# Hybrid decoder block on one core: row statistics in the opening, another background order, and two norms in one step

## The chip, the core and the metric

The kernel runs on one core of a Trainium2 chip. The metric is device time in microseconds (us) of one execution; beside the median of several executions there is one execution taken by the hardware profiler. Engines are named as the profile names them: PE (TensorE matmuls; PEld is its weight load), DVE (VectorE), ACT (ScalarE), POOL (GpSimd), SP (SyncE, whose queue issues every DMA of this kernel).

## What is computed

One decoder layer over 2048 positions of width 1024, in float32, then a final norm. Cut to what matters:

```python
h = rmsnorm(x, norm1_g)
proj = h @ w_in                       # q, k, v, g, a, and three conv parts
q, k, v, g, a, cb, cc, ch = split(proj)
log_a = log_sigmoid(a @ w_gate_up + b_gate) / 16       # forget gate
o = rmsnorm(gla_chunked(q, k, v, log_a), gla_norm_g) * silu(g)
o_conv = cb * causal_conv3(cc * ch)
x = x + concat(o, o_conv) @ w_out
h2 = rmsnorm(x, norm2_g)
x = x + (silu(h2 @ w_ffn_gate) * (h2 @ w_ffn_up)) @ w_ffn_down
return rmsnorm(x, norm_f_g)
```

`rmsnorm` divides each position's 1024 values by the root of their mean square and multiplies by a gain per column.

## The kernel before, in words

**Tiling.** Positions are cut into four blocks of 512 (`PB`), two blocks to a "half". Activations lie transposed: a tile `h[k, j]` holds 128 features (k) by the 512 positions of block j. `xt` is x in that layout, `x` the plain one, one position to a row.

**Products.** Every large matmul is done in a unit of seven products instead of eight (`PRODUCTS`, L34): a unit takes 256 output columns and two blocks, and multiplies weight combinations A11, S1, S2, A12, S3, S4, A22 with operand combinations B11, T1, T2, B21, T3, B22, T4. B11 is `h[k, 0]` for k below 4, B12 `h[k, 1]`, B21 and B22 the same for k from 4. T1 = B12 - B11, T2 = B22 - T1, T3 = B22 - B12, T4 = B21 - T2. To keep float32 precision each operand is split (`split`, L145) into a rounded part hi (ACT copy, L146) and a rest lo (DVE subtraction, L147), and each product is three matmuls per k (L328 to L330), so a product is 12 matmuls of 128x512 and a unit 84. POOL forms the weight combinations (L311 to L318). Results leave PSUM by ACT copies (`copied`, L348; `settled`, L377) and DVE additions (`plus`, L352). Within a unit the first accumulator is copied as c11 after product 1, and as c12 after product 3; the second as c22 after product 2. The third product goes on in the accumulator that c11 was copied from, the fifth in that of c12, the sixth in that of c22, so those products wait for the copies.

**The opening.** `first_stats` (L414) loads the 16 tiles of xt of blocks 0 and 1, squares each on ACT, adds the squares up per block (DVE for block 0, POOL for block 1), and `column_rstd` (L160) sums them over partitions with a matmul by ones; the result is 1/rms, repeated on all partitions, in SBUF, 128x512. `build_first` (L255) then scales each tile on DVE (`scaled`, L440), splits it, and does the first unit as eight plain products (L279 to L281): 48 matmuls for block 0 (j = 0), 48 for block 1 (j = 1). After k = 3 of j = 0 block 1's `column_rstd` is issued. Then POOL forms the T's (L288), for one k after another: T1, T2 and T4 overwrite one tile `t1` from pool "b", T3 overwrites `h[k, 1]`.

**Tiles.** Pool "t" has nine tiles of 128x512 and serves block 0's `h`, the c copies, settled results and others; pool "b" has eleven and serves block 1's `h`, the T's, and most background work. "op" has 28 split operands. A tile can be taken again when the last operation that uses its old content is done.

**Background.** While units run, `tick()` after each product takes a step of the first generator in `background`: at every tick while `hurry` is set, at every second otherwise; at `pace % 4 == 1` it takes a step of `ahead` when it takes none of background. At the start the list is: `gate_weights`, `gate(0)` (the forget gates of blocks 0 and 1: 40 matmuls at L497, eight at L513, scans on DVE), `row_stats(2)`, `row_stats(3)` (1/rms of blocks 2 and 3 from rows of x: ACT squares with an accumulated sum, L397, then small operations on 128x4, and four transposes that repeat the result on all partitions, L406 and L407), `unhurried`, `h1_ahead` (operands of the second half, stored to DRAM). `h2_ahead` (L792) does the same for the second half of the feed-forward; it waits two steps, makes one block's norm, waits two more, makes the other's.

**Who sets the order.** The program is written in that order, and a planner that simulates the five engines fixes each engine's order (`TileContext(nc, schedule_with_timeline_sim=True)`, L1096): of what its model holds ready, what stands first in the program goes first. So a later line can run ahead of an earlier one that waits; in the trace the first weight splits (L146, at 13.64 us) run ahead of the Ln of the norm (L170, at 16.78 us) that stands before them. Once fixed, each engine does its instructions in that order. `issue_after` adds an order by hand.

**Activation tables.** `Ln` and `Exp` of the norms and gates need another table in ACT than `Silu`; a load (ACT_TABLE_LOAD) takes 1.283 us in the trace. `act.preload_act_table_set` loads a set that holds both.

Of the kernel before, what the change touches and what calls it, by code (L numbers as in the profile page):

```python
# [10 lines left out]
F32 = mybir.dt.float32  # L11
# [36 lines left out]
def tile_hymba_block(ctx, tc, x, xt, win, wa, wgu, wout, wffn, wdown, wdown_first, small, out):  # L48
# [111 lines left out]
    def column_rstd(ssq, n, rb=None):  # L160

        rb = ssq if rb is None else rb
        tot = bank("tot")
        pe.matmul(tot[:], ones[:], ssq[:], start=True, stop=True)
        finish_rstd(rb, tot, n)
        return rb
# [27 lines left out]
    def unhurried():  # L194
        hurry.clear()
        yield

    def drain_background(until=lambda: False):
        while background and not until():
            step()  # L200


    def split_op(src):
        o = opp.tile([P, 2, PB], F32R, name="op", tag="op")
        split(src, o[:, 0, :], o[:, 1, :])
        return o
# [45 lines left out]
            put("B22", k, b22)  # L252
            yield

    def build_first(quad, w, later):  # L255


        ops = {b: [] for _, b in PRODUCTS}
        h, o = {}, {}
        quarters = ("A11", "A12"), ("A21", "A22")  # L260
        los = []
        for j in range(2):
            for r in range(2):
                o[r, j] = bank()
            for k in range(KD):
                with ExitStack() as stack:
                    if len(los) > 1:
                        stack.enter_context(tc.issue_after(los[-2].ins))
                    h[k, j] = quad(k, j)
                x = opp.tile([P, 2, PB], F32R, name="op", tag="op")  # L270
                los.append(split(h[k, j][:], x[:, 0, :], x[:, 1, :]))
                if (j, k) == (0, 3):
                    rbs[1] = column_rstd(later, D)
                name = ("B11", "B12")[j] if k < 4 else ("B21", "B22")[j]
                ops.setdefault(name, []).append(x)
                c = slice(k % 4 * P, (k % 4 + 1) * P)
                for r in range(2):
                    q = w[quarters[r][k // 4]]
                    pe.matmul(o[r, j][:], q[:, 0, c], x[:, 0, :], start=k == 0, stop=False)  # L279
                    pe.matmul(o[r, j][:], q[:, 0, c], x[:, 1, :], start=False, stop=False)  # L280
                    pe.matmul(o[r, j][:], q[:, 1, c], x[:, 0, :], start=False, stop=k == KD - 1)  # L281
        for k in range(4):
            t1 = bt("t1")
            b11, b12, b21, b22 = h[k, 0], h[k, 1], h[k + 4, 0], h[k + 4, 1]
            for n, y, a, b in (
                ("T1", t1, b12, b11), ("T2", t1, b22, t1), ("T3", b12, b22, b12), ("T4", t1, b21, t1)
            ):
                pool.tensor_tensor(y[:], a[:], b[:], ALU.subtract)  # L288
                ops[n].append(split_op(y[:]))
        return ops, [(r, j, o[r, j], True) for j in range(2) for r in range(2)]  # L290

    def weight_quarter(src):
# [92 lines left out]
        return s  # L385


    rbs = {}

    def row_stats(b):  # L390
        ssq = mtiny.tile([P, PT, 2], F32, name="ssq", tag="ssq")
        for t in range(PT):
            for e in range(2):
                xn = bt("xn")
                r0 = b * PB + t * P
                load(xn[:], x[r0 : r0 + P, e * PB : (e + 1) * PB])
                act.activation(xn[:], xn[:], AF.Square, accum_out=ssq[:, t, e : e + 1])  # L397
            yield
        v, l, y0 = [mtiny.tile([P, PT], F32, name=n, tag=n) for n in ("msq", "rl", "ry")]
        dve.tensor_tensor(v[:], ssq[:, :, 0], ssq[:, :, 1], ALU.add)  # L400
        dve.tensor_scalar(v[:], v[:], 1.0 / D, EPS, ALU.mult, ALU.add)
        rsqrt(v[:], v[:], l[:], y0[:])
        rb_ps = bank("rb_ps")
        for t in range(PT):
            rep = mtiny.tile([P, P], F32, name="rep", tag="rep")
            dve.tensor_copy(rep[:], v[:, t : t + 1].to_broadcast([P, P]))  # L406
            pe.transpose(rb_ps[:, t * P : (t + 1) * P], rep[:], ident[:])  # L407
        rb = bt("rb2")
        act.activation(rb[:], rb_ps[:], AF.Copy)
        store(s_rb[b][:], rb[:])  # L410

    raws, first_weights, last_load = {}, {}, []

    def first_stats():  # L414

        for j in range(2):
            for k in range(KD):
                h = bt("h") if j else tt("h")
                raws[j, k] = h
                last_load[:] = [load(h[:], xt[j, :, k, :])]  # L420
            if j == 0:
                raw = raw_weights(win[0])
        ssq = [tiny.tile([P, PB], F32, name="rb2", tag="rb") for _ in range(2)]
        for j in range(2):
            for k in range(KD):
                if k == 0:
                    act.activation(ssq[j][:], raws[j, k][:], AF.Square)
                else:
                    q = opp.tile([P, 2, PB], F32, name="q", tag="op")
                    act.activation(q[:, 0, :], raws[j, k][:], AF.Square)  # L430
                    add = pool if j else dve
                    add.tensor_tensor(ssq[j][:], ssq[j][:], q[:, 0, :], ALU.add)
            if j == 0:
                rbs[0] = column_rstd(ssq[0], D)
                for n, i in (("A11", 0), ("A21", 3), ("A12", 1), ("A22", 2)):
                    first_weights[n] = weight_quarter(raw[:, i, :])
        return ssq[1]

    def scaled(g, rb, h):
        dve.scalar_tensor_tensor(h[:], h[:], g, rb[:], ALU.mult, ALU.mult)  # L440
# [8 lines left out]
        split(raw[:], w[:, :, 0, :], w[:, :, 1, :])  # L449
        yield  # L450

    def build_h(later):


        def quad(k, j):
            return scaled(col(C_G1 + k), rbs[j], raws[j, k])

        return build_first(quad, first_weights, later)

    def h1_ahead():  # L460

# [330 lines left out]
    def h2_ahead(ssq):  # L792


        rb = []
        for j in range(2):
# [117 lines left out]
    def last_unit(src, ops, b12, y, ssq):  # L914
# [51 lines left out]


    act.preload_act_table_set("natural_log_exp_and_others")
    later = first_stats()
    load(wgu_sb[:], wgu)  # L970
    ops, first = build_h(later)
# [129 lines left out]
```

## Time and profile before

| | us |
|---|---|
| median of 3 runs | 2146.97 |
| lowest, highest | 2140.72, 2151.3 |
| the profiled execution | 2146.09 |
| its span, first to last instruction | 2144.2 |
| PE busy in the span | 2043.6 |
| DVE, ACT, POOL busy | 1452.5, 1012.1, 997.0 |

The mean granted TensorE clock of the profiled execution is 0.989 of full speed. How to read the views: in the busy time by stretch, each row gives a stretch, its length, then for each engine the busy us and the number of instructions, then the granted clock, the busy share of the DMA engines and the GB/s. In the list of waits a row reads: engine, waiting operation and line, what ended the wait, the total, how often, the longest. In the groups a row reads: line, engine, operation, output and inputs, shapes, count, then busy us and mean ns of one, then the idle time in front and what ended it. In the view of a tile or line the three numbers are the shortest, median and longest ns. In the timeline a row begins with the start and the length in us.

### The profile page before, as it was taken

Reading aid. Unit: us, or ns where it says so; the run is one execution under the profiler, and the core shown is the slowest. Engines: PE = TensorE matmul, PEld = TensorE weight load, DVE = VectorE, ACT = ScalarE, POOL = GpSimd, SP = SyncE. Lnnn points to the kernel's source line nnn. Section 1 sums busy time; section 2 is a strip of 40 time slices with the busy share of each in tenths; the row PEclk is TensorE's granted clock in tenths of the full one; section 3 lists DMA queues with packets and bytes.
Section 4 is the critical chain, followed back from the end, with each engine's and each line's share of the span. In section 5 each row is a group of like instructions: output and inputs, shape, how many; then the busy total and the mean of one; then the engine's idle time right before and its main releaser. Section 6 shows DMA issues by size and latency. Waiting matters only on the chain.

```text
span 2144.2 us, 26906 instructions
## 1 busy us (share of the span) xinstructions
PE 2043.6 (95%) x9133; PEld 1651.3 (77%) x9133; DVE 1452.5 (68%) x2034; ACT 1012.1 (47%) x1962; POOL 997.0 (46%) x714
## 2 busy tenths in 40 slices
PE   4899899999999999999999999999999999999996
PEld 2677687887888887788888887787888888887775
DVE  8849965556774486888887664554686677664554
ACT  4555434574544235555454553333454454553344
POOL 4526422122201274655655436774644654445774
PEclk9999999999999999999999999999999999999998
DMA  4259658532577884465464577689455455487662
GB/s 150 76 199 315 218 228 286 156 125 79 166 247 256 309 294 152 167 240 220 172 237 182 185 303 283 254 336 355 157 191 205 154 197 196 172 329 293 266 265 108
DMA packets 189977, 467.64 MB, mean 218 GB/s; under 512 B 19856, under 2 KB 65168, under 8 KB 180112
## 3 DMA queue, kind: packets, MB, share of 16 engines
q1 hardware_dynamic: 189840, 465.93, 59.9%
q8 instruction: 72, 1.18, 0.2%
q14 instruction: 65, 0.53, 0.1%
HBM read 297.03 MB, written 168.82 MB: 217 GB/s over the span
## 4 chain that ended last, share of the span: by engine, by line
PE 70%; DVE 11%; DMA 8%; issue 4%; ACT 3%; POOL 3%; SPq 1%; DVEq 0%; POOLq 0%; ACTq 0%
PE mm L328 20%; PE mm L330 20%; PE mm L329 19%; DVE wq L147 3%; PE mm L722 3%; PE mm L725 3%; PE mm L723 3%; DMA raw<-in_wdown_dram 2%; DVE h L440 2%; DMA raw<-in_wffn_dram 1%; DVE so L147 1%; DVE op L147 1%; DMA op<-shT 1%; DVE c L352 1%; ACT wq L146 1%
## 5 line engine op out<-in xcount | busy, mean ns | idle before, releaser
L328 PE MATMUL mm<-op,wq 128*128 128x512 f32 x2495 | 982.1, 395 | 33.0 <-ACT c L348 20.3
L330 PE MATMUL mm<-op,wq 128*128 128x512 f32 x2495 | 967.6, 392 | 12.4 <-DVE wq L147 11.2
L329 PE MATMUL mm<-op,wq 128*128 128x512 f32 x2495 | 975.6, 391 | 2.5 <-DVE op L147 2.5
L147 DVE TENSOR_TENSOR wq<-raw,wq 128x512 fp32r<-128x512 f32 (+2 forms) x628 | 536.6, 860 | 320.2 <-ACT wq L146 318.3
L146 ACT ACTIVATE wq<-raw 128x512 fp32r<-128x512 f32 (+2 forms) x628 | 367.1, 589 | 566.7 <-PE mm L330 415.4
L328 PEld LDWEIGHTS mm<-op,wq 128*128 128x128 f32 x2495 | 470.4, 189 | 152.1 <-ACT c L348 27.1
L330 PEld LDWEIGHTS mm<-op,wq 128*128 128x128 f32 x2495 | 470.5, 189 | 121.9 <-DVE wq L147 22.4
L329 PEld LDWEIGHTS mm<-op,wq 128*128 128x128 f32 x2495 | 470.7, 189 | 99.8 <-DVE op L147 3.0
L313 POOL TENSOR_TENSOR raw<-s,raw 128x512 f32<-128x512 f32 (+2 forms) x98 | 130.7, 1333 | 437.7 <-DVE wq L147 403.1
L352 DVE TENSOR_TENSOR c<-mm,c 128x512 f32<-128x512 f32 x270 | 185.1, 686 | 100.1 <-PE mm L330 98.0
L311 POOL TENSOR_TENSOR s<-raw 128x512 f32<-128x512 f32 (+2 forms) x98 | 130.8, 1335 | 207.9 <-DMA raw<-in_wffn_dram 96.1
L318 POOL TENSOR_TENSOR raw<-raw 128x512 f32<-128x512 f32 (+2 forms) x98 | 130.4, 1331 | 129.5 <-DVE wq L147 128.9
L348 ACT ACTIVATE c<-mm 128x512 f32<-128x512 f32 x270 | 156.4, 585 | 23.8 <-PE mm L330 23.0
L704 POOL TENSOR_TENSOR ssx<-ssx,q 128x512 f32<-128x512 f32 x52 | 75.2, 1459 | 151.0 <-ACT q L703 151.0
L312 POOL TENSOR_TENSOR raw<-raw 128x512 f32<-128x512 f32 (+2 forms) x98 | 137.2, 1400 | 4.6
L884 POOL TENSOR_TENSOR y<-c,y 128x512 f32<-128x512 f32 x66 | 98.6, 1496 | 67.3 <-DVE c L352 67.2
L147 DVE TENSOR_TENSOR so<-t,so 128x512 fp32r<-128x512 f32 x100 | 89.6, 902 | 23.8 <-ACT so L146 23.6
L722 PE MATMUL mm<-op,wq 128*128 128x512 f32 x256 | 100.9, 394 | 0.0
L723 PE MATMUL mm<-op,wq 128*128 128x512 f32 x256 | 99.7, 390 | 0.0
L146 ACT ACTIVATE wq<-s 128x512 fp32r<-128x512 f32 (+2 forms) x98 | 57.6, 588 | 89.2 <-PE mm L330 86.6
L147 DVE TENSOR_TENSOR wq<-s,wq 128x512 fp32r<-128x512 f32 (+2 forms) x98 | 81.9, 835 | 15.6 <-ACT wq L146 15.2
L146 ACT ACTIVATE so<-t 128x512 fp32r<-128x512 f32 x100 | 62.9, 630 | 48.6 <-DMA sa_B<-so 19.9
(177 smaller groups left out, 1931.2 us busy)
## 6 DMA issues: line engine op xcount, KB each, us to landing
raw<-in_wffn_dram SPq DMA_DIRECT2D x44, 1024.0 KB, 6.1
sa_T<-so SPq DMA_DIRECT2D x88, 512.0 KB, 4.9
op<-sa_T SPq DMA_DIRECT2D x88, 512.0 KB, 9.6
sa_B<-so SPq DMA_DIRECT2D x69, 512.0 KB, 3.4
op<-sa_B SPq DMA_DIRECT2D x69, 512.0 KB, 9.2
raw<-in_win_dram SPq DMA_DIRECT2D x24, 1024.0 KB, 5.7
raw<-in_wdown_dram SPq DMA_DIRECT2D x24, 768.0 KB, 6.1
sx<-y SPq DMA_DIRECT2D x48, 256.0 KB, 3.4
```

The source lines that it names most:

```text
L146: last_hi[:] = [act.activation(hi, src, AF.Copy)]
L147: return dve.tensor_tensor(lo, src, hi.bitcast(F32), ALU.subtract)
L311: pool.tensor_tensor(s1, a21, a22, ALU.add)
L312: pool.tensor_tensor(a21, a11, a21, ALU.subtract)
L313: pool.tensor_tensor(a11, s1, a11, ALU.subtract)
L328: pe.matmul(o[:], wh, xh, start=first and k == 0, stop=False, skip_group_check=True)
L329: pe.matmul(o[:], wh, xl, start=False, stop=False, skip_group_check=True)
L330: return pe.matmul(o[:], wl, xh, start=False, stop=k == n - 1, skip_group_check=True)
L348: act.activation(t[:], o[:], AF.Copy)
L352: dve.tensor_tensor(t[:], o[:], t[:], ALU.add)
L722: pe.matmul(o[e, j][:], wh, m[:, 0, :], start=k == 0, stop=False)
L723: pe.matmul(o[e, j][:], wh, m[:, 1, :], start=False, stop=False)
```

## The change

1. *Opening.* `first_loads` takes the place of `first_stats`: it loads the rows of x of a block (four loads of 128x1024) ahead of the block's xt, and splits the first weight load in four. The mean square comes from one ACT square per row tile with an accumulated sum (`row_squares`), and `rows_rstd`, cut out of `row_stats`, gives 1/rms in a PSUM bank, from which `scaled` reads it. Block 1's squares are issued beside k = 4 to 7 of j = 0, its `rows_rstd` after k = 7.
2. *T operands.* The loop over the four T's is now the outer one, k the inner; T1, T2 and T4 overwrite `h[k, 0]` (pool "t") instead of `t1`.
3. *Background order.* `gate_weights`, six empty steps, `row_stats(2)`, `row_stats(3)`, `gate(0)`, `unhurried`, `h1_ahead`. `row_stats` loads one row tile ahead.
4. *Second feed-forward operands.* `h2_ahead` waits one step, preloads the table, and makes both norms in one step.

The diff, cut to its core:

```diff
+    def pause(n):
+        for _ in range(n):
+            yield
...
-                if (j, k) == (0, 3):
-                    rbs[1] = column_rstd(later, D)
+                if j == 0 and k >= PT:
+                    row_squares(1, k - PT)
...
-        for k in range(4):
-            t1 = bt("t1")
-            b11, b12, b21, b22 = h[k, 0], h[k, 1], h[k + 4, 0], h[k + 4, 1]
-            for n, y, a, b in (
-                ("T1", t1, b12, b11), ("T2", t1, b22, t1), ("T3", b12, b22, b12), ("T4", t1, b21, t1)
-            ):
-                pool.tensor_tensor(y[:], a[:], b[:], ALU.subtract)
-                ops[n].append(split_op(y[:]))
+            if j == 0:
+                rbs[1] = rows_rstd(squares[1])
+        for n, y, a, b in (
+            ("T1", (0, 0), (0, 1), (0, 0)), ("T2", (0, 0), (4, 1), (0, 0)),
+            ("T3", (0, 1), (4, 1), (0, 1)), ("T4", (0, 0), (4, 0), (0, 0)),
+        ):
+            for k in range(4):
+                yy, aa, bb = [h[k + dk, j] for dk, j in (y, a, b)]
+                pool.tensor_tensor(yy[:], aa[:], bb[:], ALU.subtract)
+                ops[n].append(split_op(yy[:]))
...
     def row_stats(b):
         ssq = mtiny.tile([P, PT, 2], F32, name="ssq", tag="ssq")
-        for t in range(PT):
-            for e in range(2):
-                xn = bt("xn")
+
+        def fetch(t):
+            xs = [bt("xn") for _ in range(2)]
+            for e, xn in enumerate(xs):
                 r0 = b * PB + t * P
                 load(xn[:], x[r0 : r0 + P, e * PB : (e + 1) * PB])
+            return xs
+
+        nxt = fetch(0)
+        yield
+        for t in range(PT):
+            xs = nxt
+            if t + 1 < PT:
+                nxt = fetch(t + 1)
+            for e, xn in enumerate(xs):
                 act.activation(xn[:], xn[:], AF.Square, accum_out=ssq[:, t, e : e + 1])
             yield
+        dve.tensor_tensor(ssq[:, :, 0], ssq[:, :, 0], ssq[:, :, 1], ALU.add)
+        rb = bt("rb2")
+        act.activation(rb[:], rows_rstd(ssq)[:], AF.Copy)
+        store(s_rb[b][:], rb[:])
+
+    def rows_rstd(ssq):
+
         v, l, y0 = [mtiny.tile([P, PT], F32, name=n, tag=n) for n in ("msq", "rl", "ry")]
...
             pe.transpose(rb_ps[:, t * P : (t + 1) * P], rep[:], ident[:])
...
+        return rb_ps
...
+    def row_squares(b, t):
+        act.activation(rows[b, t], rows[b, t], AF.Square, accum_out=squares[b][:, t, 0:1])
+
+    def first_loads():
+
+        raw = rawp.tile([P, 4, PB], F32, name="raw", tag="raw")
+        for b in range(2):
+            squares[b] = mtiny.tile([P, PT, 2], F32, name="ssq", tag="ssq")
+            for t in range(PT):
+                xr = opp.tile([P, 2 * PB], F32, name="xr", tag="op")
+                rows[b, t] = xr[:]
+                r0 = b * PB + t * P
+                load(xr[:], x[r0 : r0 + P, :])
             for k in range(KD):
-                h = bt("h") if j else tt("h")
...
+                if b == 0 and k % 4 == 0:
+                    for i in ((0, 3), (1, 2))[k // 4]:
+                        raw_loads.append(load(raw[:, i, :], win[0][:, i, :]))
+                h = bt("h") if b else tt("h")
+                raws[b, k] = h
+                last_load[:] = [load(h[:], xt[b, :, k, :])]
+        for t in range(PT):
+            row_squares(0, t)
+        rbs[0] = rows_rstd(squares[0])
...
     def h2_ahead(ssq):
 
 
-        rb = []
-        for j in range(2):
-            for _ in range(2):
-                yield
-            rb.append(column_rstd(ssq[j], D))
+        yield
+        act.preload_act_table_set("natural_log_exp_and_others")
+        rb = [column_rstd(ssq[j], D) for j in range(2)]
+        yield
...
-        [gate_weights(), gate(0, ops), row_stats(2), row_stats(3), unhurried(), h1_ahead()]
+        [
+            gate_weights(), pause(6), row_stats(2), row_stats(3), gate(0, ops), unhurried(),
+            h1_ahead(),
+        ]
```

More of the change, by code (lines that the diff above doesn't have):

```diff
@@ L407, in row_stats @@
             pe.transpose(rb_ps[:, t * P : (t + 1) * P], rep[:], ident[:])
[L408 to L414, printed above, removed]
-        for j in range(2):
-            for k in range(KD):
-                h = bt("h") if j else tt("h")
[L419 to L437, printed above, removed]
@@ new lines, in rows_rstd @@
+        return rb_ps
+    rbs, raws, first_weights, last_load, rows, squares = {}, {}, {}, [], {}, {}
+    def row_squares(b, t):
[9 more added lines that the diff above has]
+                load(xr[:], x[r0 : r0 + P, :])
+            for k in range(KD):
+                if b == 0 and k % 4 == 0:
[7 more added lines that the diff above has]
+        rbs[0] = rows_rstd(squares[0])
+        for n, i in (("A11", 0), ("A21", 3), ("A12", 1), ("A22", 2)):
+            first_weights[n] = weight_quarter(raw[:, i, :])
```

15 lines of the change are left out of this document (6 added, 9 removed).

## The prediction, made before the changed kernel ran

> **What bounds the kernel now.** I read the page's first part for the engine that fills the span, then the busy time by stretch to find where that engine is not fed.
>
> ```profile
> PE 2043.6 (95%) x9133; PEld 1651.3 (77%) x9133; DVE 1452.5 (68%) x2034; ACT 1012.1 (47%) x1962; POOL 997.0 (46%) x714
> ```
> ```profile
> core 0: us, PE busy (x) PEld busy (x) DVE busy (x) ACT busy (x) POOL busy (x), PEclk, DMA share, GB/s
> 0.00:26.00 26.00, 2.10 (x3) 0.53 (x3) 15.88 (x24) 14.42 (x24) 9.85 (x13) 1.00 0.78 288
> 26.00:42.40 16.40, 14.47 (x50) 10.45 (x50) 16.20 (x20) 5.75 (x10) 5.46 (x4) 1.00 0.00 0
> 42.40:63.00 20.60, 16.40 (x64) 11.20 (x63) 20.33 (x20) 8.12 (x14) 13.74 (x9) 1.00 0.07 27
> 63.00:74.00 11.00, 3.67 (x8) 1.83 (x7) 8.73 (x7) 5.11 (x10) 9.77 (x7) 0.69 0.16 60
> 74.00:112.00 38.00, 38.00 (x148) 28.09 (x147) 31.55 (x53) 25.88 (x58) 15.07 (x10) 0.96 0.38 132
> 112.00:160.00 48.00, 43.14 (x179) 34.49 (x178) 19.91 (x43) 21.74 (x49) 10.81 (x8) 0.93 0.54 183
> ...
> 823.00:892.00 69.00, 61.42 (x265) 49.09 (x264) 47.10 (x57) 38.33 (x60) 31.29 (x22) 1.00 0.30 112
> ```
>
> TensorE is the bound at large, so an edit is worth what it takes off TensorE's waits. They are concentrated at the start: 26 us with no product, then two stretches in which DVE is full (16.20 of 16.40, 20.33 of 20.60), then 11 us with 8 matmuls at a granted clock of 0.69. The waits name the releasers:
>
> ```profile
> PE tot L164 <- DVE rb L432: 12.9, 1, 12.9
> PE mm L279 <- ACT op L146: 11.7, 2, 11.0
> PE mm L280 <- DVE op L147: 4.7, 7, 1.5
> PE mm L328 <- ACT c L348: 4.4, 1, 4.4
> PE mm L329 <- DVE op L147: 2.5, 1, 2.5
> ```
>
> The first two lines are the column statistics, the third the operand splits, the last two the T operands of the second unit. All are what the change touches.
>
> **The change, part by part.** The timeline gives the opening's dates and TensorE's pace.
>
> ```profile
> 9.14 2.59 ACT L430 ACTIVATE q<-h 128x512 f32<-128x512 f32 x4 [0.29 <-DMA h<-in_xt_dram]
> ...
> 25.98 1.22 PE L279 MATMUL mm<-op,wq 128*128 128x512 f32 x2 [10.96 <-ACT op L146]
> ...
> 29.69 0.63 PE L280 MATMUL mm<-op,wq 128*128 128x512 f32 x1
> 30.12 0.63 PE L281 MATMUL mm<-op,wq 128*128 128x512 f32 x1
> ...
> 33.04 0.39 PE L280 MATMUL mm<-op,wq 128*128 128x512 f32 x1
> 33.27 0.39 PE L281 MATMUL mm<-op,wq 128*128 128x512 f32 x1
> ```
>
> A matmul starts every 0.23 us, and every 0.43 us up to 33 us.
>
> *Step 1, the start.* Removed: 16 squares, 14 adds and the wide Ln-Exp-Newton chain that ends in L440 at 23.6. Added: eight row loads of 512 KB, eight squares and two chains on 128x4. The closest rows are those of the row statistics that blocks 2 and 3 use already:
>
> ```profile
> L397 ACT ACTIVATE xn<-xn x16: 617/628/636, 104.6 to 138.6; 128x512 f32<-128x512 f32 x16
> L397 ACT ACTIVATION_READ_ACCUMULATOR xn<-xn x16: 184/188/203, 105.1 to 139.1; 128x1 f32 x16
> ```
> ```profile
> L406 DVE COPY rep<-msq x8: 216/222/227, 116.3 to 148.5; 128x128 f32<-128x128 f32 x8
> ...
> L151 ACT ACTIVATE rl<-msq x2: 194/200/206, 112.5 to 141.3; 128x4 f32<-128x4 f32 x2
> ```
>
> Block 0's rows are 2.1 MB, first on the queue. The old 2.1 MB of xt were being squared until 11.7 (9.14 + 2.59), so I take 9.3 for the last row tile. Its square has twice the elements of a 0.63 us one: 1.1, plus 0.19 for the accumulator: 10.6. Then some 1.2 for six small operations at about the 0.20 of L151 (mean, Ln, Exp, three Newton steps), and 1.4 for four copies of 0.22 and their transposes: 13.2. One scaling (0.75) and one hi split (0.63) later TensorE starts at 14.6 instead of 26.0: **-11.4**. Bounds: if the rows land by 7.5 it is 13; if they take the old squares' full 11.7 and the hops are double, 18. So -13 to -8.
>
> *Step 2, first half of the first unit.* The 48 matmuls need 11.0 us plus a slow start of 14 or so at 0.43 (+2.8). DVE needs eight scalings, eight lo splits and two weight splits. What they take depends on POOL:
>
> ```profile
> L440 DVE SCALAR_TENSOR_TENSOR h<-h,sml,rb x16: 739/1192/1777, 23.6 to 55.3; 128x512 f32<-128x512 f32 x16
> ...
> L147 DVE TENSOR_TENSOR op<-h,op x16: 677/683/1782, 26.9 to 59.9; 128x512 fp32r<-128x512 f32 x16
> ```
> ```profile
> L683 DVE SCALAR_TENSOR_TENSOR osb<-ot,sml,gt x16: 741/746/751, 327.7 to 698.5; 128x512 f32<-128x512 f32 x16
> ```
>
> With both operands in SBUF the scaling takes 0.74 or, beside a POOL add, up to 1.78; the same operation with one operand in PSUM (L683) never left 0.74 to 0.75. The change leaves rb in PSUM and takes POOL's square sums out, so 8 x (0.75 + 0.68) + 2 x 0.68 = 12.8, under TensorE's 13.8. I take 14.2 against 16.4: **-2.2** (0 to -2.7), ending at 28.8. The table of the Trainium skill, VectorE: DVE Perf Modes, section Rules for kernel authors, speaks against this: for many operations on a matmul's output it would copy it to SBUF first, PSUM being the 1x case. Were SBUF operands read at twice that rate, the 16 scalings would cost 6 us less than I count (an estimate from that page); the trace disagrees for this form (0.739 at best in SBUF, 0.741 in PSUM).
>
> *Step 3, second half.* Block 1's rows and xt end at 9.4 MB; the first 26 us moved 288 GB/s, which puts their end at 33 us, and since that mean holds the slow begin and an idle end, perhaps at 27. The scalings use them from 29 to 42. For them, and for the second 128x4 chain, which closes the first half where the old one lay inside it, I add 1 us of wait. The old 20.6 us hold 64 matmuls, 16 of them of the next unit (3.7), so 16.9 for this half; eight scalings at 0.75 instead of some 1.2 save 3.6. 16.9 - 3.6 + 1 = 14.3: **-2.6** (+1 to -5), ending at 43.1.
>
> *Step 4, the T operands.* Same 16 subtractions and 16 splits, other order and other places:
>
> ```profile
> L288 POOL TENSOR_TENSOR t<-h,t 128x512 f32<-128x512 f32 x8 | 13.6, 1705 | 13.9 <-DVE op L147 13.9
> L288 POOL TENSOR_TENSOR t<-h 128x512 f32<-128x512 f32 x4 | 6.8, 1714 | 11.8 <-DVE h L440 11.8
> ```
>
> POOL waits 13.9 us because each step of a k overwrites the tile whose split must be done. With k innermost three other k's lie between, so the wait goes and all four T1 come first. Late next is the tile pool: now T1, T2 and T4 live in the first block's h, so eight of its nine t tiles stay taken until T4, where four used to come free at T1. The second unit's c copies need such tiles: c11 gets the ninth after the four settled results, c22 and c12 wait for T4 of k=0. On ACT the hi splits stand behind such a copy. By 1.7 us each: T1 done by 40, T2 49, T3 56, three weight sums of POOL between, first T4 at 60, last at 66, its split at 68. TensorE has three or four products to do from 43.1 (2.8 each), then waits for c12 until 62.5, then does three to 70.9. Before, at 112 us TensorE had done this unit plus 84 other matmuls:
>
> ```profile
> L328 PE MATMUL mm<-op,wq 128*128 128x512 f32 x40 | 16.6, 415 | 4.8 <-ACT c L348 4.4 <-ACT op L146 0.5
> ...
> L497 PE MATMUL a_ps<-op,wa_sb 128*128 128x512 f32 x40 | 11.8, 440 | 0.0
> L513 PE MATMUL z<-a_sb,wgu_sb 64*128 64x512 f32 x8 | 4.2, 628 | 0.0
> ```
>
> 3 x 40 products less the 84 of this unit, and 48 of the gate, are 84: at 0.23 that is 19.3, so 92.7 is the like date. 92.7 - 70.9 = 21.8, of which steps 1 to 3 are 16.2 and this step **-5.6**. Ends: without the tile wait 180 matmuls from 14.6 end at 59 (-18); with every T in a row, +12 (rival 3). Two corrections of equal size: gate or third-unit products can be set into the hole (-3), and the hole halves the clock (+3). For the latter the row is 63:74 at 0.69 and 74:112 at 0.96, so 2 x (0.31 x 11 + 0.04 x 38) = 10 us at half rate, 5 us lost; I charge 3 for a shorter hole. The Trainium skill, TensorE: Matmul & The Clock Gate, Part 1, gives about 3.4 us of work to come back to full clock, so 1.7 us lost; by it the sum would be 1.3 lower, but the row stayed slow for longer.
>
> *Step 5, order behind it.* Row statistics of blocks 2 and 3 move ahead of the gate, with 16 loads of 256 KB, one store and one load each on SP's queue, two fetched ahead. They need b tiles, eight of eleven of which hold block 1's h until T3, so they start about 56. The gate's four wide groups on DVE come later:
>
> ```profile
> L525 DVE TENSOR_TENSOR_SCAN g<-ones,g 128x128 f32<-128x128 f32 x16 | 8.5, 585 | 0.0
> ...
> L519 DVE TENSOR_SCALAR g<-z,sml 128x512 f32<-128x512 f32 x4 | 2.9, 740 | 0.0
> L529 DVE TENSOR_TENSOR g<-g 128x512 f32<-128x512 f32 x4 | 2.7, 682 | 0.0
> L522 DVE TENSOR_TENSOR g<-g,g 128x512 f32<-128x512 f32 x4 | 2.7, 672 | 0.0
> ```
>
> They sum to 17 us. Cover: DVE idles 28 of the 48 us of 112:160. Without it, up to 17 us more where DVE leads. Its ACT, PE and four stores move along. I take **+2.5** (0 to +17).
>
> *Step 6, the second operands' norms.* Before, in 823:892:
>
> ```profile
> L384 ACT ACT_TABLE_LOAD x3 | 3.8, 1283 | 0.1
> ...
> L170 ACT ACT_TABLE_LOAD x2 | 2.6, 1283 | 0.0
> L171 ACT ACT_TABLE_LOAD x2 | 2.6, 1283 | 0.0
> ```
> ```profile
> PE mm L330 <- DVE wq L147: 5.6, 2, 3.2
> ```
>
> Seven loads, of which one is silu's own; both norms together leave three. Five us less of ACT, in a stretch where TensorE waits 5.6 for weight splits: **-2.5** (0 to -5).
>
> Sum: -11.4 - 2.2 - 2.6 - 5.6 + 2.5 - 2.5 = -21.8. The profiled execution took 2146.09 (span 2144.2), so 2124; the median of the three runs, 2146.97 (2140.72 to 2151.3), lies 0.9 above: **2125**.
>
> **Rivals.**
> 1. *TensorE paced throughout.* The t tiles don't hold it, because results leave faster or the gate fills the hole: step 4 then gives its end of -18, 12.4 more, **2112**. For: 48 gate and 84 third-unit matmuls are there to fill. Against: c12 is needed within the unit.
> 2. *Given back.* The gate's 17 us and the earlier h1 splits meet in stretches where DVE is full, and the opening's gain is stretched out again: -21.8 + 17 = about -5, **2143**. Against: the 28 idle us.
> 3. *Slower: the T chain runs in a row.* DVE, ACT and POOL take their queues in order; if the nine t tiles and those queues make each T cost POOL 1.7, hi 0.63, lo 1.7 in sequence (4 us), 16 of them from 33 end at 97, the three weight sums push it to 102, and 2.8 to 5 follow: 106 against 92.7, +13, and five for a halved clock, less 2.5: **2162**. It outweighs the earlier start if the last T split falls after some 88 us, and costs 0.5% from about 98. Against: the four k's are independent.
>
> The change missing its aim is a rival for step 6 only (the preload may land ahead of a silu): 2.5 us, inside the range.
>
> **Numbers.** Forecast 2125 with its own range 2114 to 2136: 0.58; rival 1 0.15; rival 2 0.16; rival 3 0.11. 0.5% is 10.7 us, about what a measurement of this kernel can tell from no change. Faster: 0.58 + 0.15 = 0.73; same 0.16; slower 0.11. The range reaches from rival 1's lower side, 2108, over rival 2 to 2148; outside are rival 3 and the tail of rival 1.
>
> **What would show it.** First L279 matmul near 14.6 (12 to 18); scalings at 0.75 throughout; 28.8 and 43 as the ends of the two halves; a TensorE wait for a c copy between 50 and 63, and the last T split at 68; three table loads near 850. A first matmul after 20, or a T split after 88, makes the forecast wrong; so does DVE full from 100 to 160.

## The result

| | before | after |
|---|---|---|
| median of 11 runs each, us | 2146.97 | 2156.24 |
| lowest, highest, us | 2140.24, 2151.3 | 2151.5, 2162.19 |
| the profiled execution, us | 2146.09 | 2151.5 |
| its span, us | 2144.2 | 2149.8 |

The ratio of after to before is 1.0049, with a 95% interval of 1.0035 to 1.0062: the change makes the kernel slower by half a per cent, where 1% faster was forecast. 2156.24 lies above the range. The profiled execution of after is the fastest of its eleven, so its trace shows the loss at its smallest.

The first part of the page of after; the order of the engines is that of the line shown of before.

```profile
PE 2048.1 (95%) x9137; PEld 1655.0 (77%) x9137; DVE 1429.1 (66%) x2035; ACT 1004.7 (47%) x1960; POOL 980.7 (46%) x707
```

Every engine but PE (with its weight loads) has less to do than before, and the span is 5.6 us longer: the totals tell nothing of the loss. The busy time by stretch of after, in the stages of its own opening (first product, end of the first unit's first half, and so on):

```profile
0.00:19.26 19.26, 1.34 (x4) 0.65 (x4) 6.33 (x21) 9.23 (x17) 1.11 (x7) 1.00 0.88 298
19.26:35.90 16.64, 14.98 (x52) 11.33 (x52) 12.20 (x25) 9.54 (x19) 0.51 (x1) 1.00 1.03 396
35.90:56.00 20.10, 17.11 (x66) 11.76 (x67) 20.07 (x20) 14.90 (x36) 18.87 (x12) 1.00 0.31 106
56.00:80.00 24.00, 13.54 (x41) 8.91 (x40) 23.90 (x27) 11.17 (x22) 15.91 (x11) 0.79 0.13 47
80.00:112.00 32.00, 32.00 (x144) 26.40 (x143) 12.53 (x21) 14.43 (x33) 10.34 (x8) 1.00 0.53 186
112.00:160.00 48.00, 47.25 (x196) 35.47 (x195) 32.17 (x62) 25.53 (x51) 12.89 (x8) 1.00 0.42 136
160.00:200.00 40.00, 36.01 (x149) 29.06 (x150) 35.84 (x40) 23.07 (x40) 22.20 (x14) 0.96 0.91 318
```

The waits of TensorE in after up to 112 us, beside those of before in the prediction:

```profile
PE rb_ps L428 <- DVE rep L427: 15.5, 2, 15.3
PE mm L336 <- DVE wq L147: 7.1, 3, 3.4
PE mm L283 <- ACT op L146: 4.0, 2, 2.5
PE mm L335 <- DVE op L147: 3.7, 4, 1.4
```

The first of these rows is the norm's transposes, which wait for the statistics. The first product comes at 19.26 instead of 25.98. The wait for a c copy (4.4) is gone, but two waits for DVE's lo splits, of weights (wq) and of operands (op), stand in its place. From 36 to 80 DVE is full (20.07 of 20.10, 23.90 of 24.00), and in the second of these stretches TensorE gets through 41 matmuls only. To see who is ahead, add up the matmuls. Before's rows up to 160 us come to 452 (3, 50, 64, 8, 148, 179); the first six of these come to 503. Both have the gate behind them by then, so after leads by 51 matmuls, and at 0.23 us each that is 11.7 us. Forecast for the opening and the background order together was 19.3.

Now the same count over the rest. The busy time by stretch of before, then of after:

```profile
0.00:811.00 811.00, 752.65 (x3534) 602.20 (x3535) 560.28 (x898) 389.45 (x843) 267.15 (x181) 0.99 0.60 208
811.00:880.00 69.00, 66.68 (x291) 54.10 (x290) 45.12 (x59) 39.61 (x61) 29.18 (x21) 1.00 0.35 130
880.00:1140.00 260.00, 253.90 (x1112) 207.78 (x1111) 218.42 (x248) 130.21 (x230) 149.70 (x97) 1.00 0.56 209
```
```profile
0.00:811.00 811.00, 762.80 (x3592) 611.19 (x3592) 554.33 (x912) 390.48 (x852) 261.29 (x177) 0.99 0.63 216
811.00:880.00 69.00, 62.55 (x251) 49.86 (x252) 47.67 (x58) 37.16 (x59) 33.52 (x24) 0.93 0.33 119
880.00:1140.00 260.00, 244.98 (x1058) 199.49 (x1057) 193.42 (x233) 124.24 (x222) 127.15 (x87) 0.99 0.56 202
```

At 811 us after is 58 matmuls ahead (13.3 us); at 880 it is 18 ahead (4.1 us); at 1140 it is 36 behind (8.3 us). The opening did gain. What it gained, and more, is lost in the first 330 us of the feed-forward. Of the change only step 6 edits that part, though not all of the loss turns out to be its own. The waits of TensorE from 880 to 1140 show most of it; before, then after:

```profile
PE mm L328 <- ACT c L348: 0.6, 2, 0.3
```
```profile
PE mm L334 <- ACT c L354: 14.0, 5, 4.9
```

TensorE waits 14.0 us for copies of results (`copied`), where before waited 0.6. One of these waits, as ACT's timeline shows it; the bracket at the end is the idle time in front of the instruction and what ended it:

```profile
1041.71 0.63 ACT L146 ACTIVATE so<-h 128x512 fp32r<-128x512 f32 x1 [0.83 <-DMA shT<-so]
1045.24 0.63 ACT L146 ACTIVATE so<-t 128x512 fp32r<-128x512 f32 x1 [2.90 <-DMA sa_T<-so]
1048.34 0.63 ACT L146 ACTIVATE so<-t 128x512 fp32r<-128x512 f32 x1 [2.46 <-DMA sa_T<-so]
1048.88 0.58 ACT L390 ACTIVATE sg<-mm 128x512 f32<-128x512 f32 x1
...
1049.87 0.59 ACT L354 ACTIVATE c<-mm 128x512 f32<-128x512 f32 x1
```

The hi splits named `so` belong to background work that is stored to DRAM (`store_split`): sa_T are the T values of the feed-forward units (`split_later`), shT those of the next half's operands (`combine` in `h2_ahead`). There are three `so` tiles, and a split must wait until an older tile's store has landed. ACT does its queue in order, so the silu and the copies behind the two waiting splits start at 1048.9 and 1049.9, and TensorE waits 4.9 us for the second of them. In all, from 880 to 1140 the `so` splits of after wait 39.8 us on ACT for stores, those of before 24.5.

### The profile page after: what moved, and what is told of

The parts are those of the page before. It is cut to its first block, busy times and chain, and to the rows that moved or that the text cites. A ratio compares the mean times of both kernels' runs of the same rounds, so it can differ in the third digit from the quotient of the medians.

```text
span 2149.8 us, 26968 instructions
## 1 busy us (share of the span) xinstructions
PE 2048.1 (95%) x9137; PEld 1655.0 (77%) x9137; DVE 1429.1 (66%) x2035; ACT 1004.7 (47%) x1960; POOL 980.7 (46%) x707
## 4 chain that ended last, share of the span: by engine, by line
PE 74%; DVE 11%; DMA 7%; issue 3%; ACT 3%; POOL 1%; SPq 0%; DVEq 0%; ACTq 0%; POOLq 0%
PE mm L334 21%; PE mm L336 21%; PE mm L335 21%; DVE wq L147 3%; PE mm L742 2%; PE mm L743 2%; PE mm L745 2%; DVE op L147 2%; DVE h L460 2%; DMA shT<-so 1%; DMA op<-sa_B 1%; DMA raw<-in_wdown_dram 1%; DMA sa_T<-so 1%; PE a_ps L517 1%; DVE so L147 1%
## 5 line engine op out<-in xcount | busy, mean ns | idle before, releaser
L147 DVE TENSOR_TENSOR wq<-raw,wq 128x512 fp32r<-128x512 f32 (+2 forms) x628 | 523.5, 838 | 304.4 <-ACT wq L146 301.4
L147 DVE TENSOR_TENSOR so<-t,so 128x512 fp32r<-128x512 f32 x100 | 87.6, 876 | 36.8 <-ACT so L146 36.7
L147 DVE TENSOR_TENSOR wq<-s,wq 128x512 fp32r<-128x512 f32 (+2 forms) x98 | 84.1, 858 | 16.1 <-ACT wq L146 15.6
```

Source lines behind the costliest of these rows:

```text
L147: return dve.tensor_tensor(lo, src, hi.bitcast(F32), ALU.subtract)
```

## The experiments

The theory after the first look: the opening's parts gain, and step 6 costs more than they gain, because with it the operand steps of `h2_ahead` begin two steps sooner. The rivals: the gate moved behind gives the gain back (rival 2 of the prediction); or the norms themselves, merged, are in the way. Each ratio below is against runs of before taken beside that kernel, whose medians lie between 2145.76 and 2147.54.

**All but step 6, and step 6 alone.** `e1_opening_alone` is the changed kernel with the old `h2_ahead`, `e2_norms_alone` the kernel before with the new one.

```diff
-        yield
-        act.preload_act_table_set("natural_log_exp_and_others")
-        rb = [column_rstd(ssq[j], D) for j in range(2)]
-        yield
+        rb = []
+        for j in range(2):
+            for _ in range(2):
+                yield
+            rb.append(column_rstd(ssq[j], D))
```

> Everything of the change but step 6: the second operands' norms are as before. Theory A (the norms' edit costs the feed-forward some 18 us, the opening gains some 13): about 2134, below the kernel before by 0.4 to 0.7%, and TensorE waits for c copies in 880:1140 drop from 14.0 us to about 1. Rival B (any change of the opening shifts the planner's order of the feed-forward, and that drift is the loss): 2150 to 2156, the c waits stay.

> The kernel before with the new h2_ahead only. Theory A: 2160 to 2168, with TensorE waits of some 10 us more in the stretch around the two norms and some 12 us for c copies later. Rival B: 2144 to 2150, within 0.15% of the kernel before.

Measured: 2141.61, 0.9972 (0.9958 to 0.9985), and 2162.14, 1.0071 (1.0058 to 1.0083). By their ratios these are -6.0 and +15.2 us; the sum, 9.2, is near the change's own (10.5 by its ratio, 9.3 by the medians). The c waits of `e1_opening_alone` fell to 0.7 as expected, but it gained less than the forecast 2134. The waits of `e2_norms_alone` from 880 to 1140:

```profile
PE mm L328 <- ACT c L348: 12.9, 4, 4.6
```

So step 6 does harm without any of the rest.

**Place or merging.** `e3_norms_late` merges the norms but leaves the operand steps where they were (three empty steps ahead of the norms); `e4_norms_first` puts the norms into the first step and leaves the operand steps where the change has them.

```diff
 e3:
-        yield
+        for _ in range(3):
+            yield
         act.preload_act_table_set("natural_log_exp_and_others")
 e4:
-        yield
         act.preload_act_table_set("natural_log_exp_and_others")
         rb = [column_rstd(ssq[j], D) for j in range(2)]
         yield
+        yield
```

> The changed kernel, but the step with both norms comes after three empty steps, so that the operand steps behind it begin where they did before. If the loss in 880:1140 comes from the place of the operand steps (so splits in front of the silu and c copies on ACT), the c waits there go and the time falls by about 12, to 2144; the some 10 us around the norms stay or move with them. If it comes from doing both norms in one step, nothing falls: 2152 to 2158.

> The changed kernel, but both norms come in the first step (in the program ahead of the first silu) and the operand steps stay where the change put them. If the four table loads in a row behind the first silu are the price of 811:880, they go (no load at L170 or L171 before 900) and the time falls by 5 to 10, to 2146 to 2151, with the c waits of 880:1140 unchanged. If the tables are hidden and the place of the operand steps is all, nothing changes: 2153 to 2159.

Measured: 2143.63, 0.9981 (0.997 to 0.9992), and 2154.65, 1.0036 (1.0025 to 1.0048). TensorE's waits for c copies between 880 and 1140 are 0.6 and 13.0 us. Merging the norms does nothing that can be measured (`e3` against `e1`), and neither does their place (`e4` against after); where the operand steps begin decides. The expectation that the table loads would vanish in `e4` failed: six remain.

**Only the operand steps put back.** `e9_operands_late` is the changed kernel with two more empty steps behind the norms, `e10_operands_between` with one.

```diff
         rb = [column_rstd(ssq[j], D) for j in range(2)]
         yield
+        yield
+        yield
```

> The changed kernel with both norms where the change put them, and two more empty steps behind them, so that only the operand steps begin where they did in the kernel before. If the place of the operand steps is the cause: c waits in 880:1140 under 3 us and 2141 to 2146, as with both moved. If the place of the norms is: c waits of 12 to 16, 2152 to 2158.

> The same with one more empty step, so that the operand steps begin halfway between the two. If the loss goes with the place step by step: c waits between 3 and 12 us in 880:1140 and a time between 2143 and 2155. If every earlier place is alike: as the changed kernel, 2152 to 2158.

Measured: 2138.3, 0.9955 (0.9941 to 0.9968), and 2142.15, 0.9984 (0.9971 to 0.9996). The waits of `e9_operands_late` in the same stretch:

```profile
PE mm L334 <- ACT c L354: 1.1, 3, 0.5
```

Its `so` splits wait 23.4 us for stores on ACT, after's 39.8. Two empty steps turn 0.49% slower into 0.45% faster. One step already takes the waits for c copies down to 1.7 us (`e10_operands_between`), so the loss doesn't shrink evenly from step to step, and neither of its expectations held.

**Why two steps.** `ahead` steps fall on every fourth tick, and an operand's seven steps repeat after 28 ticks; a pair of feed-forward units, whose seven values `split_later` stores, has 14 ticks. If it is the coincidence of the two streams of stores that costs, the pattern repeats every seven steps. `e12_plus_seven` has the changed kernel's phase one such turn later, `e13_plus_nine` that of `e9_operands_late`.

```diff
         rb = [column_rstd(ssq[j], D) for j in range(2)]
-        yield
+        for _ in range(8):      # e13: range(10)
+            yield
```

> The changed kernel with seven more empty steps behind the norms (nine were between norm and operands are not meant; it is seven beyond the change, five beyond e9_operands_late). Operand steps fall on every fourth tick and their own pattern repeats every seven steps, 28 ticks; two pairs of feed-forward units are also 28 ticks. So this kernel has the phase of the changed kernel, one k (28 ticks, about 80 us) later. Theory 1, phase: waits of TensorE for c copies between 960 and 1220 us total 10 to 15 us as in the changed kernel, ratio 1.002 to 1.006. Theory 2, absolute place: those waits are below 4 us, ratio 0.9945 to 0.9975 as in e9_operands_late.

> The changed kernel with nine more empty steps behind the norms: the phase of e9_operands_late, seven steps later in place. Both theories expect waits for c below 4 us between 960 and 1220 us and a ratio of 0.994 to 0.998; it is the control for e12_plus_seven. If it is as slow as e12_plus_seven while e9_operands_late is not, being late by itself costs (operands that are not ready for the second half), and e12_plus_seven tells nothing of the phase.

Measured: 2153.93, 1.0035 (1.0024 to 1.0046), and 2140.88, 0.9978 (0.9965 to 0.999). So it is the phase, not the place. TensorE's timeline of after, the matmuls that waited over 1 us for a c copy from 880 on:

```profile
887.36 0.50 PE L334 MATMUL mm<-op,wq 128*128 128x512 f32 x1 [2.97 <-ACT c L354]
...
969.12 0.50 PE L334 MATMUL mm<-op,wq 128*128 128x512 f32 x1 [2.94 <-ACT c L354]
...
1050.51 0.80 PE L334 MATMUL mm<-op,wq 128*128 128x512 f32 x1 [4.86 <-ACT c L354]
...
1132.89 0.50 PE L334 MATMUL mm<-op,wq 128*128 128x512 f32 x1 [2.42 <-ACT c L354]
```

And of `e12_plus_seven`:

```profile
957.67 0.50 PE L334 MATMUL mm<-op,wq 128*128 128x512 f32 x1 [2.94 <-ACT c L354]
...
1040.63 0.79 PE L334 MATMUL mm<-op,wq 128*128 128x512 f32 x1 [4.84 <-ACT c L354]
...
1121.66 0.50 PE L334 MATMUL mm<-op,wq 128*128 128x512 f32 x1 [2.99 <-ACT c L354]
...
1202.43 0.50 PE L334 MATMUL mm<-op,wq 128*128 128x512 f32 x1 [2.41 <-ACT c L354]
```

Four waits again, of nearly the same sizes in another order, 81 to 83 us apart, which is two pairs of units (336 matmuls at 0.23, 77 us) and the wait itself. Counted by matmuls of the units, neighbours stand exactly 336 apart in both traces, and the first of `e12_plus_seven` stands where the second of after does: the whole row is one turn later, with one wait for each of the four k's of `h2_ahead`. (In microseconds it is 70 and not 80 later, since this kernel is some 11 us ahead of after at that point.) In `e13_plus_nine` the same stretch (960 to 1220 us) has 1.1 us of them in all.

**The number of `so` tiles.** `e5_four_so` has a fourth; to make room, pool "fx" goes from 11 tiles to 9. `e5b_nine_general` is the control, with nine and three.

```diff
-        for n, bufs in (("fx", 11), ("fo", 3))
+        for n, bufs in (("fx", 9), ("fo", 4))     # e5b: ("fx", 9), ("fo", 3)
```

> The changed kernel with four instead of three tiles for stored feed-forward operands (so), and nine instead of eleven in the general pool to make room. Theory: in 880:1140 ACT stands at a hi split that waits for one of the three so tiles to be stored, with the silu and c copies behind it, and TensorE waits 14 us for c. With four tiles the c waits there fall under 4 us and the time by about 10, to 2146. Rival: the order on ACT is the cause and the tile count is not: c waits stay at 12 to 16 us, time 2152 to 2160.

> Control for the run with four so tiles: the changed kernel with nine tiles in the general pool and three so tiles. If the two general tiles matter little: 2150 to 2162 and c waits of 12 to 16 us in 880:1140.

Measured: 2144.49, 0.9997 (0.9984 to 1.001), waits for c 5.4 us; the control, in one run, 2148.56, waits 7.3 us. The control, expected at 12 to 16 us of waits, moved nearly as far; why nine "fx" tiles alone do so is not shown. Between the two, the fourth tile halves what the `so` splits wait for stores on ACT (880 to 1140: 37.9 us with three, 19.7 with four), but TensorE's waits for c fall only from 7.3 to 5.4. So a fourth tile as a cure is not shown either way; four beside eleven was not tried.

**The background order.** `e6_gate_ahead` is `e1_opening_alone` with the gate ahead of the row statistics again.

```diff
-            gate_weights(), pause(6), row_stats(2), row_stats(3), gate(0, ops), unhurried(),
-            h1_ahead(),
+            gate_weights(), gate(0, ops), row_stats(2), row_stats(3), unhurried(), h1_ahead(),
```

> The opening alone, but with the background order of the kernel before (gate ahead of the row statistics, no empty steps). If the moved gate costs what the lead loses between 115 and 200 us (13 us like for like at the middle of the third unit, 6 at the sixth): about 6 less than the opening alone, 2135, and no TensorE wait of over 3 us for a c copy in 160:175. If the loss there is that of the h1 splits on a full DVE, whatever the gate does: 2139 to 2145.

Measured: 2145.38, 0.9997 (0.9985 to 1.0008), against 0.9972 with the new order. The intervals meet at their ends, so the new order is no loss, and by the medians worth 4 to 5 us. Neither expectation held: the time is above both, and TensorE waits 4.4 us for a c copy between 160 and 175 with the gate ahead too. The trace says less than the medians: this profiled execution is the fastest of its twelve, has 532 matmuls done at 160 where `e1_opening_alone` has 498, loses half of that lead by 200 (131 against 148 in the stretch), and ends 2 us sooner.

**The order of the T's.** `e8_t_by_k` is `e1_opening_alone` with k as the outer loop again, in the new tiles.

```diff
-        for n, y, a, b in (...):
-            for k in range(4):
+        for k in range(4):
+            for n, y, a, b in (...):
```

> The opening alone, but the T's are again formed for one k after the other (in the same tiles). By step 4 the new loop order is worth some 5 us, since four T1 come first: 2146 to 2149, TensorE waits for op splits at S1 x T1 longer by 4 or more. Rival: the t tiles are what holds the unit, and they come free earlier by k: same or faster, 2136 to 2142.

Measured: 2152.99, 1.003 (1.0017 to 1.0043): 11 us slower than with the new order. About half of this is the opening's: the third silu that reads PSUM (`sg`) starts at 438.38 in `e1_opening_alone` and at 443.73 here, 5.4 us later, the last at 1878.27 and 1883.83. Of the 9.6 us between the two profiled spans the rest comes behind that, for reasons that the traces don't tie to the T's. POOL's group of the subtractions from 30 to 120 us, of after and then of `e8_t_by_k`; behind the second bar stands POOL's idle time in front of them:

```profile
L294 POOL TENSOR_TENSOR h<-h 128x512 f32<-128x512 f32 x16 | 25.2, 1597 | 37.0 <-DVE h L460 33.6 <-DVE op L147 2.7 <-DVE msq L158 0.7
```
```profile
L294 POOL TENSOR_TENSOR h<-h 128x512 f32<-128x512 f32 x16 | 24.8, 1561 | 44.8 <-DVE h L460 30.7 <-DVE op L147 12.2 <-DVE ssq L414 1.2
```

POOL's wait for splits (DVE op) is 2.7 with the new order, 12.2 with the old.

**The norm ahead of the weights.** `e7_norm_first` is `e1_opening_alone` with the first two weight splits held behind the norm's Exp and last repeat, and the next two behind the third scaled tile.

```diff
-        for n, i in (("A11", 0), ("A21", 3), ("A12", 1), ("A22", 2)):
-            first_weights[n] = weight_quarter(raw[:, i, :])
+        first_raw.append(raw)
+        with tc.issue_after(last_exp[0].ins), tc.issue_after(last_rep[0].ins):
+            for n, i in (("A11", 0), ("A21", 3)):
+                first_weights[n] = weight_quarter(raw[:, i, :])
...
+                if (j, k) == (0, 2):
+                    with tc.issue_after(last_hi[0].ins), tc.issue_after(los[-1].ins):
+                        for n, i in (("A12", 1), ("A22", 2)):
+                            w[n] = weight_quarter(first_raw[0][:, i, :])
```

> The opening alone, with the first weight splits put behind the norm: two behind the Exp on ACT and the last row copy on DVE, two behind the third tile's split. In the changed kernel the norm's Ln and the first scaling stand behind weight splits that wait for their loads, and the first product comes at 19.3 instead of the forecast 14.6. If that order is the missed part of step 1: first product at 15 to 17, lead at the third unit up by 2 to 4 us, time 2138 to 2140. Rival: the unit's T operands set the date, and the earlier start is lost in the wait for them: first product earlier, lead at the third unit as before, 2140 to 2143.

Measured: 2136.74, 0.9951 (0.9938 to 0.9963). Its timeline:

```profile
11.23 0.20 ACT L151 ACTIVATE rl<-msq 128x4 f32<-128x4 f32 x1 [0.24 <-DVE msq L426]
...
14.71 1.41 DVE L466 SCALAR_TENSOR_TENSOR h<-h,sml,rb_ps 128x512 f32<-128x512 f32 x2
...
16.18 1.22 PE L287 MATMUL mm<-op,wq 128*128 128x512 f32 x2 [2.05 <-ACT op L146]
```

The first product comes 3.1 us sooner than in after, and sooner than in any of the twelve traces with the change's start (17.33 to 19.57); the end comes 4.9 us sooner than in `e1_opening_alone`.

**Both repairs.** `e11_both_mended` is `e7_norm_first` with the `h2_ahead` of `e9_operands_late`; its edit is those two.

> The changed kernel with both repairs found so far: the first weight splits issued behind the norm (as in e7_norm_first) and the operand steps of the second feed-forward half begun two steps later (as in e9_operands_late). Theory that the two losses are separate places and add up: 0.9951 x 0.9955 / 0.9972 (the last being the opening alone, which both contain) = 0.9934, about 2133 us, first product at 16.2 us, TensorE waits for c copies between 880 and 1140 us below 2 us. Rival, that one repair shifts the background so that the other is lost again: 0.9955 to 0.997 (2137 to 2141), with waits for c above 4 us in that stretch or a T split later than 80 us.

Measured: 2136.98, 0.9952 (0.9936 to 0.9968). Its first product is at 16.29, its waits for c from 880 to 1140 are 0.7 us, so both repairs hold; yet the median is that of `e7_norm_first`, and the theory that the two gains add up to 2133 failed. The gain of the merged norms over the old ones, 0.17% between `e1` and `e9`, was within the two intervals and did not come again. The best that was reached is half a per cent below before.

## Why the prediction was wrong

31.2 us lie between 2125 and 2156.24. Of these, some 17.7 are step 6 (+15.2 alone, forecast -2.5) and 13.3 are steps 1 to 5 (-6.0, forecast -19.3).

**The step that failed is step 6:** "both norms together leave three", "Five us less of ACT", -2.5, where +15.2 was measured. Without it the time is 2141.61, inside the range. It priced the norms and not what follows them in the same generator. With one step ahead of the norms and one behind, where before had four in all, every operand step moves two steps forward, and that puts their stores onto those of the feed-forward units: 14.0 us of waiting for c copies where before had 0.6. The prediction's own rule, that ACT does its queue in order, was applied to the T operands only; its bound of 0 to -5 left no room for a loss. Nor did the loads come down to three. ACT's timeline of after:

```profile
829.34 0.63 ACT L390 ACTIVATE c<-c 128x512 f32<-128x512 f32 x1
829.99 1.28 ACT L170 ACT_TABLE_LOAD   x1
831.28 0.69 ACT L170 ACTIVATE l<-tot,eps 128x512 f32<-128x512 f32 x1
831.99 1.28 ACT L171 ACT_TABLE_LOAD   x1
833.29 0.63 ACT L171 ACTIVATE y<-l 128x512 f32<-128x512 f32 x1
834.46 1.28 ACT L170 ACT_TABLE_LOAD   x1
```

Ln (L170) and Exp (L171) each load their own table, twice, right behind a silu (L390): the preload had no effect here, which the prediction had named as possible. There are six loads in this stretch of after against seven. The Trainium skill, ScalarE: Activation LUTs, section Table sets: the hidden batching unit, counts Ln followed by Exp as one load, both being in one set; this trace loads between them each time. By that rule step 6 would have saved some 3.9 us more of ACT (an estimate: three of the measured 1.28 us loads), still far from its loss.

**Step 1** was right in its way and mis-sized: -6.7 instead of -11.4 (the other eleven traces with this start begin between 17.33 and 19.57). The row squares end at 11.27 (forecast 10.6), but the norm does not come next. The timeline of after:

```profile
11.08 0.19 ACT L434 ACTIVATION_READ_ACCUMULATOR xr<-xr 128x1 f32 x1
...
13.06 0.63 ACT L146 ACTIVATE wq<-raw 128x512 fp32r<-128x512 f32 x1 [1.28 <-DMA raw<-in_win_dram]
13.60 0.19 ACT L151 ACTIVATE rl<-msq 128x4 f32<-128x4 f32 x1
...
16.54 1.29 ACT L146 ACTIVATE wq<-raw 128x512 fp32r<-128x512 f32 x2 [2.51 <-DMA raw<-in_win_dram]
17.20 0.69 DVE L147 TENSOR_TENSOR wq<-raw,wq 128x512 fp32r<-128x512 f32 x1 [0.98 <-ACT wq L146]
17.81 1.40 DVE L460 SCALAR_TENSOR_TENSOR h<-h,sml,rb_ps 128x512 f32<-128x512 f32 x2
```

The Ln stands behind a weight split that waits for its load, and the first scaling behind the lo split of another. The change cuts that weight load in four and queues its halves among the xt tiles, so the splits are late, and in-order queues pass that on. `e7_norm_first`, which takes the splits out of the way, bears it out.

**Step 2** held: the 48 matmuls run from 19.26 to 33.55, 14.3 us (forecast 14.2), and the scalings with rb in PSUM take 0.74 beside POOL.

**Step 3** failed: the second half's last plain product ends at 55.2, 21.6 us after the first half's; in before it was 20.3 (42.7 to 63.0). Both have 13 matmuls of the second unit among them, not 16, so this half became 1.4 us longer where 2.6 shorter was forecast. The second chain costs 2.4 us until the next product (35.95), not 1; and POOL, which no longer waits, begins the T's inside this half (busy 18.87 of 20.10), so that 11 lo splits (L147, op) average 1.29 us instead of 0.68. What the scalings save, the splits lose, and more.

**Step 4** was right about the order of the T's and wrong about the whole. The chain by T is worth some 5 us in the opening against the one by k (`e8`), where 5.6 was forecast. But its dates were 12 us too early (last T split at 80, not 68), because DVE is full from 36 to 80; TensorE waits for DVE's splits and not, as forecast, for a t tile. After ends the second unit at 86.5, not 70.9, with as many matmuls done as before has at 92.7, the prediction's own like date. So steps 1 to 4 gave 6.2 us and not 21.8. The T's themselves are done 17 us sooner than in before (80.1 against 97.1), but before fills the time with the gate's matmuls (74 to 98), and after, whose gate comes from 120 on, gets through only 41 matmuls from 56 to 80.

**Step 5** forecast +2.5 and the runs show no loss (`e6`). From 86.5 to 160 the lead grows from 6.2 to 11.7 us: TensorE is busy 72.75 of these 73.5 us. Of rival 2's two mechanisms the gate is not borne out. Nor do the earlier h1 splits take the gain for good: from 160 to 200 the lead falls from 51 matmuls to 32 (149 against 168), but DVE is as busy there in before (37.48 of 40, after 35.84), and at 811 the lead is 58.

The rest of the opening's gain goes where the feed-forward begins, with the old norms too: `e1_opening_alone` leads by 44 matmuls at 811 and by 16 at 880. The first stretch of it, in before, in after and in `e1_opening_alone`:

```profile
811.00:830.00 19.00, 16.68 (x74) 13.50 (x73) 15.17 (x20) 9.89 (x18) 10.37 (x7) 1.00 0.44 166
```
```profile
811.00:830.00 19.00, 15.44 (x54) 11.91 (x55) 10.73 (x13) 9.90 (x18) 9.64 (x8) 0.82 0.37 135
```
```profile
811.00:830.00 19.00, 15.50 (x56) 12.16 (x55) 11.83 (x15) 9.63 (x16) 8.57 (x6) 0.82 0.30 111
```

In both changed kernels TensorE waits 3.5 us for a lo split of a weight, in before 2.3, and the granted clock of the stretch is 0.82 instead of 1.00. Dated by the same product, the lead of `e1_opening_alone` falls from 9.1 us to 5.0 between 818 and 832, and it is 4.5 at the last silu. (The count at 880 also holds a wait of 2.0 us for DVE that before has behind 880.) No term of the prediction has this place. Why the wait is longer, and why the clock falls in these traces and not in before, was not tried.

One slip in the prediction's sums changed nothing: rival 2's comes to 2142, not 2143.

## What to carry to other kernels

A background step that is removed moves everything behind it in its generator: ask which stores, splits and waits now fall beside which of the foreground, and whether the two patterns have a common period, for then one clash comes back in every turn. On an engine that works in order, a split that waits for a buffer or for its load holds up whatever urgent copy or norm stands behind it; look for the bracket on the background instruction, not on the copy. When a change has several parts, run each alone: here a gain of 6 and a loss of 15 would have passed as one small loss.

## What the hardware showed beside

DVE operations with both operands in SBUF stretch beside a busy POOL, small ones by as much as large ones. From the timeline of after:

```profile
14.34 0.15 DVE L156 TENSOR_TENSOR rl<-ry 128x4 f32<-128x4 f32 x1
...
57.97 1.73 POOL L317 TENSOR_TENSOR s<-raw 128x512 f32<-128x512 f32 x1
...
58.48 1.24 DVE L414 TENSOR_TENSOR ssq<-ssq 128x4 f32<-128x4 f32 x1
...
67.12 1.26 DVE L156 TENSOR_TENSOR rl<-ry 128x4 f32<-128x4 f32 x1
```

The first stands where POOL is all but idle (1.11 us busy up to 19.26). The one at 58.48 ends at 59.72, POOL's operation beside it at 59.70. So it is with all ten stretched operations on 128x4 in this trace (0.72 to 1.26 us): each ends 0.02 to 0.03 us after a POOL operation, while the 77 that overlap none took at most 0.17. The twelve stretched lo splits of operands (128x512) of the opening end 0.54 to 0.55 us after one, most of their own 0.68. In this trace, then, such an operation looks held until POOL's ends, and not slowed. The scalings with rb in PSUM took 0.734 to 0.747 throughout. Four small operations between 58 and 70 us cost DVE 4.9 us where 0.6 would be looked for, in the stretch in which TensorE waits for DVE.
